# Moving an in-place difference, a copy and a block of zeros in a matmul with logsumexp

## The chip, the cores and the metric

The kernel runs on one core of a Trainium2 chip. The metric is the device time of one execution in microseconds; of several runs the median is taken. A profiled execution gives, beside its time, the span from its first to its last instruction and a record of every instruction on each engine: TensorE (PE, its weight loads shown as PEld), VectorE (DVE), ScalarE (ACT), GpSimd (POOL) and SyncE (SP).

## The reference

```python
def setup_inputs():
    m, k, n = 1024, 4096, 4096
    return {
        "a": np.random.randn(m, k).astype(np.float32),
        "b": np.random.randn(k, n).astype(np.float32),
    }

def reference(a, b):
    x = np.matmul(a, b)
    return special.logsumexp(x, axis=-1).astype(np.float32)
```

A product of 1024 x 4096 by 4096 x 4096, of which only the logarithm of the sum of exponentials of each row is kept: 1024 numbers.

## The kernel before

**Tiles.** The 1024 rows are 8 row tiles of 128 (MT). K is 32 tiles of 128, taken in 16 pairs (KP): the two tiles of a pair are the two K halves of a 2x2 split. The 4096 columns are 8 blocks (NB) of 512 (FD), each split into two halves of 256 (H). Both inputs are loaded as f32 and turned to f16 by the loading DMA, issued by POOL. Each load of a block of b is cut into four groups of four K pairs (G, GI).

**Block 0** (column block 0) is computed in the ordinary way while a streams in. Pieces of a land in slots of the buffer tb, PE transposes them (L169), DVE and ACT take turns in copying the transposed pieces to aT (L180, L182), and `plain` multiplies them (L187) as soon as both sides are there. Beside this DVE forms sums of parts of a: s1 = A11+A22, s2 = A21+A22, s5 = A11+A12 (`a_sums_early`), and later, in place in aT, A21-A11 and A12-A22 (`a_sums_late`). At the very start `warm` issues filler matmuls on a block of zeros (L257), which lies in a part of s5 that isn't written yet; they produce nothing that is used.

**Blocks 1 to 7** use Strassen's seven products in place of eight. A *quad* is a pair of row tiles by one column block: four quads (MP) per block. The result of a quad lies in two PSUM tiles: r0 holds C11 and C12 side by side, r1 holds C21 and C22. The sums of parts of b are made by DVE once for each block, by the methods of `Block`, group by group:

| name | value | where |
|---|---|---|
| T1 | B11+B22 | tb |
| T4 | B21-B11 | tb |
| T6 | B11+B12 | tb |
| T7 | B21+B22 | in place of B21 |
| T3 | B12-B22 | in place of B12 |

In each quad PE runs M1 = s1 T1 into c11, M5 = s5 B22 into c12, M2 = s2 B11 into c21, M6 = (A21-A11) T6 into c22, then M7 = (A12-A22) T7 added to c11, M3 = A11 T3 added to c12, and M4 = A22 T4 added to c21, 16 matmuls of 256 columns each (L332). Before M7, M3 and M4 add to their PSUM halves, ACT has to copy what stands there: M1 and M5 together (L382, to e), M2 (L387, to s). After M3 and M4 ACT copies again (L420, L422), DVE subtracts and adds the copies crosswise (L78, L81), and takes the maximum of each row (L84). The exponentials with their sums (ACT, L89) wait in the list `pending` and are issued by `flush()` in the next quad, between the copies of M1, M5 and of M2.

The first two quads of block 1 are *joint*: their M1, M5, M2 and M6 are issued together, group by group, since the sums of block 1 come one group at a time. Each then goes its own way with M7, M3, M4. The second of them has a buffer e of its own.

**The turn from one block to the next.** In the last quad of a block (`tail`) DVE makes the next block's sums. T1 is issued before the additions of that quad, T6 before its M7, and T4, T7, T3 at the end, behind its maxima. T6 reads B12, T4 reads B21: T3 and T7 overwrite these, and so come later.

**Order.** The order of the instructions on every engine is the order of the program (a manual schedule); each engine works through its own queue in order, and a wait of one instruction holds up all that is queued behind it on the same engine.

The places that matter for the change, by name: `zeros` (L259) and `warm`; the choice of e (L347); the copies at L382 and L387; the tail's T6 (L416); and the tail's last loop (L433).

Of the kernel before, what the change touches and what calls it, by code (L numbers as in the profile page):

```python
# [13 lines left out]
def kernel(  # L14
# [6 lines left out]
    nc = tc.nc  # L21
    P = 128
    FD = 512
    H = FD // 2
    f32 = mybir.dt.float32
# [9 lines left out]
    MP, KP = MT // 2, KT // 2  # L35
    SC = 1024
    KC, JT = K // SC, SC // P
    G = 4
# [7 lines left out]
    fix_pool = ctx.enter_context(tc.tile_pool(name="fix", bufs=1))  # L46
# [9 lines left out]
            name=nc.get_next_instruction_name(),  # L56
# [10 lines left out]
    s5 = cst_pool.tile([P, KP, MP, P], f16, name="s5")  # L67
# [9 lines left out]
    def add(o, x, y):  # L77
        nc.vector.tensor_tensor(out=o, in0=x, in1=y, op=ALU.add)  # L78

    def sub(o, x, y):  # L80
        nc.vector.tensor_tensor(out=o, in0=x, in1=y, op=ALU.subtract)  # L81

    def lse_max(pt, m, nb):
        nc.vector.tensor_reduce(  # L84
            out=negmax[:, m, nb : nb + 1], in_=pt, axis=AX.X, op=ALU.max, negate=True
        )

    def lse_exp(pt, m, nb):
        nc.scalar.activation(  # L89
            out=pt,  # L90
            in_=pt,
            func=AF.Exp,
            bias=negmax[:, m, nb : nb + 1],
            scale=1.0,
            accum_out=tsum[:, m, nb : nb + 1],
        )

    def load_b(nb, g, parts=1):
        bt = bt_pool.tile([P, GI, 2, FD], f16, name=f"b_{nb}_{g}", tag="bt")
        step = 2 * GI // parts  # L100
        flat = bt.rearrange("p i t n -> p (i t) n")
        rows = b.rearrange("(k p) n -> p k n", p=P)
        for h in range(parts):
            nc.gpsimd.dma_start(  # L104
                out=flat[:, h * step : (h + 1) * step],
                in_=rows[:, g * 2 * GI + h * step : g * 2 * GI + (h + 1) * step, ts(nb, FD)],
            )
        return bt
# [33 lines left out]
    def acc_tiles(name):  # L142
        return [
            psum_pool.tile([P, FD], f32, name=f"acc_{name}_{h}", tag="ps")
            for h in range(2)
        ]
# [49 lines left out]
    def a_sums_early(r, q):  # L196
        a11, a12 = aT[:, r, 0, q, 0, :], aT[:, r, 1, q, 0, :]
        a21, a22 = aT[:, r, 0, q, 1, :], aT[:, r, 1, q, 1, :]
        add(s1[:, r, q], a11, a22)
        add(s2[:, r, q], a21, a22)  # L200
        add(s5[:, r, q], a11, a12)

    def a_sums_late(r, q):
        a11, a12 = aT[:, r, 0, q, 0, :], aT[:, r, 1, q, 0, :]
        a21, a22 = aT[:, r, 0, q, 1, :], aT[:, r, 1, q, 1, :]
        sub(a21, a21, a11)
        sub(a12, a12, a22)
# [48 lines left out]
        for _ in range(n):  # L256
            nc.tensor.matmul(acc[2][1], zeros[:, 0:P], zeros[:, 0:FD], start=True, stop=True)  # L257

    zeros = s5[:, 0].rearrange("p q c -> p (q c)")  # L259
    nc.vector.memset(zeros[:, 0:FD], 0.0)  # L260
    warm(10)
    blk = Block(1)
# [45 lines left out]
    def flush():  # L308
        for f in pending:
            f()  # L310
        pending.clear()

    for nb in range(1, NB):
        nxt = None
        if nb + 1 < NB:
            nxt = Block(nb + 1)
            for g in range(G):
                nxt.raw.append(load_b(nb + 1, g))
        quads = {}
        for q in range(MP):  # L320
            if q not in quads:

                both = (0, 1) if nb == 1 and q == 0 else (q,)
                for p in both:
                    quads[p] = acc_tiles(f"{nb}_{p}")
            r0, r1 = quads[q]
            c11, c12 = r0[:, 0:H], r0[:, H:FD]
            c21, c22 = r1[:, 0:H], r1[:, H:FD]

            def product(c, lhs, rhs, start=False, g=None):  # L330
                for i in range(KP) if g is None else range(g * GI, (g + 1) * GI):
                    nc.tensor.matmul(  # L332
                        c,
                        lhs(i),
                        rhs(i),
                        start=(start and i == 0),
                        stop=(i == KP - 1),
                        skip_group_check=True,
                    )

            first, tail = nb == 1 and q < 2, nxt is not None and q == MP - 1
            final = nxt is None and q == MP - 1


            s = fix_pool.tile([P, 4, H], f32, name=f"s_{nb}_{q}", tag="s")
            x, e = s[:, 1::2], s[:, 0:2]
            if final or (first and q == 1):  # L347
                e = fix_pool.tile([P, 2, H], f32, name=f"e_{nb}_{q}", tag="e")

            def m1(c, p=q, **k):  # L350
                product(c, lambda i: s1[:, i, p], lambda i: T1[:, i], **k)

            def m5(c, p=q, **k):
                product(c, lambda i: s5[:, i, p], lambda i: blk.b(i, 1, 1), **k)

            def m2(c, p=q, **k):
                product(c, lambda i: s2[:, i, p], lambda i: blk.b(i, 0, 0), **k)

            def m6(c, p=q, **k):
                product(c, lambda i: aT[:, i, 0, p, 1], lambda i: T6[:, i], **k)  # L360

            def m7(c, **k):
                product(c, lambda i: aT[:, i, 1, q, 0], lambda i: blk.b(i, 1, 0), **k)

            def m3(c, **k):
                product(c, lambda i: aT[:, i, 0, q, 0], lambda i: blk.b(i, 0, 1), **k)

            def m4(c, **k):
                product(c, lambda i: aT[:, i, 1, q, 1], lambda i: T4[:, i], **k)

            if first and q == 0:
                for g in range(G):
                    for p in both:
                        u0, u1 = quads[p]
                        m1(u0[:, 0:H], p=p, start=True, g=g)
                        m5(u0[:, H:FD], p=p, g=g)
                        m2(u1[:, 0:H], p=p, start=True, g=g)
                        m6(u1[:, H:FD], p=p, g=g)
            elif not first:
                m1(c11, start=True)  # L380
                m5(c12)
            nc.scalar.copy(out=e, in_=r0.rearrange("p (h n) -> p h n", h=2))  # L382
            flush()
            if not first:
                m2(c21, start=True)
                m6(c22)
            nc.scalar.copy(out=s[:, 2], in_=c21)  # L387
            if tail:
                for g in range(G):
                    nxt.do_t1(g)  # L390
            add(s[:, 2], s[:, 2], e[:, 1])
            sub(s[:, 0], s[:, 2], e[:, 0])
            if final:

                z = psum_pool.tile([P, FD], f32, name="z", tag="ps")[:, 0:H]
                y = e[:, 0]
                m3(c12)
                nc.scalar.copy(out=x[:, 0], in_=c12)
                nc.scalar.copy(out=y, in_=c11)
                m4(c21)  # L400
                nc.scalar.copy(out=x[:, 1], in_=c21)
                m7(z, start=True)
                sub(x[:, 0], x[:, 0], s[:, 0])
                sub(y, y, s[:, 2])
                lse_max(c12, 2 * q, nb)
                lse_exp(c12, 2 * q, nb)
                add(c22, c22, x[:, 0])
                lse_max(r1, 2 * q + 1, nb)
                lse_exp(r1, 2 * q + 1, nb)
                add(y, y, x[:, 1])  # L410
                add(z, z, y)
                lse_max(z, 2 * q, NB)
                lse_exp(z, 2 * q, NB)
                continue
            if tail:
                for g in range(G):  # L416
                    nxt.do_t6(g)
            m7(c11)
            m3(c12)
            nc.scalar.copy(out=x[:, 0], in_=c12)  # L420
            m4(c21)
            nc.scalar.copy(out=x[:, 1], in_=c21)  # L422
            sub(x, x, s[:, 0::2])
            add(c22, c22, x[:, 0])
            add(c11, c11, x[:, 1])
            rows = (r0, r1)
            for h in range(2):
                lse_max(rows[h], 2 * q + h, nb)
                pending.append(lambda h=h, q=q, nb=nb, rows=rows: lse_exp(rows[h], 2 * q + h, nb))
            if first and q == 1:  # L430
                a_sums_early(slice(0, KP), MP - 1)
                a_sums_late(slice(0, KP), MP - 1)
            if tail:  # L433
                for f in (nxt.do_t4, nxt.do_t7, nxt.do_t3):
                    for g in range(G):
                        f(g)
        blk = nxt
# [42 lines left out]
```

## Time and profile before

| what | value |
|---|---|
| median of three runs | 440.37 us (439.47 to 440.76) |
| profiled execution, its own time | 438.74 us |
| its span | 436.8 us |
| granted TensorE clock | 0.999 |
| PE busy | 426.1 us, 98% of the span |
| DVE busy | 228.2 us, 52% |
| ACT busy | 109.6 us, 25% |
| first product of block 1 | 83.7 us after the start |
| moved by DMA | 42.48 MB |

How to read it: the spans and starts given below are microseconds from the first instruction of the profiled execution. Matmuls are pipelined, so the duration of one runs over the start of the next; distances between starts are the better measure. The profile names a tile by its name in the program and a buffer number; several names are shortened in it: s_69, s_70 and s_71 are s1, s2 and s5; acc_0_0 and acc_0_1 are r0 and r1 of quad 0 of a block, acc_1_0 and acc_1_1 those of quad 1, and so on, and b_0 to b_3 are the four groups of a block of b.

### The profile page before, as it was taken

What the parts mean: (1) busy time and instruction counts of PE and PEld (TensorE: products, weight loads), DVE (VectorE), ACT (ScalarE), POOL (GpSimd) and SP (SyncE); (2) the same over time, 40 slices, a digit from 0 to 9 for tenths busy, and PEclk for the clock granted to TensorE, in tenths of its full rate; (3) what the DMA queues carried; (4) which work ended last, traced back from release to release, by engine and by line L of the source; (5) the groups of instructions that cost most, each with busy time, mean ns of one, the idle gap of its engine ahead of it and who ended that gap; (6) DMA issues with size and microseconds to landing.
All of it is one profiled execution on the core that took longest, in us unless ns stands there. A gap on an engine that the chain in (4) does not pass through costs nothing.

```text
span 436.8 us, 8377 instructions
## 1 busy us (share of the span) xinstructions
PE 426.1 (98%) x3679; PEld 349.3 (80%) x3679; DVE 228.2 (52%) x434; ACT 109.6 (25%) x262; POOL 54.0 (12%) x84
## 2 busy tenths in 40 slices
PE   7999999999999999999999999999999999999995
PEld 3455555687888888888888888888888888888884
DVE  0336456943868533683358632693348722693324
ACT  2121226203222211222222212222222122222223
POOL 7444440200003000300003000300003000000000
PEclk9999999999999999999999999999999999999999
DMA  8999999998009910397009920298008930000000
GB/s 130 208 208 207 208 209 207 207 207 141 2 0 161 208 21 0 50 207 132 2 0 146 207 36 0 36 207 146 2 0 130 207 52 0 2 2 2 0 2 1
DMA packets 38260, 42.48 MB, mean 97 GB/s; under 512 B 1360, under 2 KB 34128, under 8 KB 38224
## 3 DMA queue, kind: packets, MB, share of 16 engines
q0 software_dynamic: 38080, 41.95, 57.1%
q8 instruction: 28, 0.46, 0.4%
q14 instruction: 8, 0.07, 0.0%
q1 hardware_dynamic: 144, 0.00, 0.0%
HBM read 83.89 MB, written 0.00 MB: 192 GB/s over the span
## 4 chain that ended last, share of the span: by engine, by line
PE 94%; DMA 2%; ACT 1%; DVE 1%; POOL 1%; issue 0%; POOLq 0%; DVEq 0%
PE acc_0_0_2998 L332 2%; PE acc_0_0_3538 L332 2%; PE acc_0_0_2458 L332 2%; PE acc_0_0_1378 L332 2%; PE acc_0_0_4070 L332 2%; PE acc_0_0_1918 L332 2%; PE acc_1_0_836 L332 2%; PE acc_1_79 L187 2%; PE acc_2_0_4326 L332 2%; PE acc_3_0_3382 L332 2%; PE acc_2_0_1634 L332 2%; PE acc_3_0_3922 L332 2%; PE acc_2_0_3794 L332 2%; PE acc_3_0_2842 L332 2%; PE acc_1_0_2586 L332 2%; PE acc_3_0_2302 L332 2%
## 5 line engine op out<-in xcount | busy, mean ns | idle before, releaser
L332 PEld LDWEIGHTS <-aT 128*128 128x128 f16 x1792 | 175.2, 98 | 25.6 <-issue 5.5
L332 PEld LDWEIGHTS <-s_69 128*128 128x128 f16 x448 | 43.8, 98 | 5.3
L332 PEld LDWEIGHTS <-s_70 128*128 128x128 f16 x448 | 43.8, 98 | 5.1
L332 PEld LDWEIGHTS <-s_71 128*128 128x128 f16 x448 | 43.8, 98 | 5.1
L187 PEld LDWEIGHTS <-aT 128*128 128x128 f16 x256 | 23.7, 98 | 24.8 <-ACT aT L182 1.2
L180 DVE COPY aT<-tps_84 128x1024 f16<-128x1024 f16 x16 | 11.1, 691 | 42.2 <-PE tps_84 L169 42.2
L182 ACT COPY aT<-tps_85 128x1024 f16<-128x1024 f16 x16 | 16.2, 1011 | 53.4 <-PE tps_85 L169 53.4
L169 PEld LDWEIGHTS <-tb 128*128 128x128 f16 x256 | 17.0, 98 | 10.1 <-DMA tb<-in_a_dram 3.0
L158 POOL DMA_DIRECT2D tb<-in_a_dram x32 | 17.5, 548 | 21.1 <-DMA tb<-in_a_dram 12.1
L257 PE MATMUL acc_1_83<-s_71 128*128 128x512 f16 x31 | 9.8, 461 | 1.9 <-DVE s_71 L260 1.2
L81 DVE TENSOR_TENSOR aT<-aT 128x512 f16<-128x512 f16 (+1 forms) x26 | 11.3, 481 | 0.0
L169 PE MATMUL tps_85<-ident,tb 128*128 128x128 f16 x128 | 9.8, 219 | 1.3 <-DMA tb<-in_a_dram 1.3
L169 PE MATMUL tps_84<-ident,tb 128*128 128x128 f16 x128 | 9.9, 220 | 0.4 <-DMA tb<-in_a_dram 0.4
L257 PEld LDWEIGHTS <-s_71 128*128 128x128 f16 x31 | 3.1, 112 | 5.9 <-issue 2.2
L104 POOL DMA_DIRECT2D b_0_1910<-in_b_dram x1 | 0.9, 881 | 46.0 <-PE acc_3_0_1762 L332 46.0
L104 POOL DMA_DIRECT2D b_0_2450<-in_b_dram x1 | 0.9, 878 | 46.1 <-PE acc_3_0_2302 L332 46.1
L104 POOL DMA_DIRECT2D b_0_3530<-in_b_dram x1 | 0.9, 878 | 46.1 <-PE acc_3_0_3382 L332 46.1
L104 POOL DMA_DIRECT2D b_0_2990<-in_b_dram x1 | 0.9, 878 | 46.0 <-PE acc_3_0_2842 L332 46.0
L104 POOL DMA_DIRECT2D b_0_1370<-in_b_dram x1 | 0.9, 873 | 45.0 <-PE acc_3_0_1222 L332 45.0
L78 DVE TENSOR_TENSOR s_71<-aT 128x512 f16<-128x512 f16 (+1 forms) x13 | 6.3, 481 | 0.0
L78 DVE TENSOR_TENSOR s_70<-aT 128x512 f16<-128x512 f16 (+1 forms) x13 | 6.3, 481 | 0.0
L78 DVE TENSOR_TENSOR s_69<-aT 128x512 f16<-128x512 f16 (+1 forms) x13 | 6.2, 478 | 0.0
(1008 smaller groups left out, 851.3 us busy)
## 6 DMA issues: line engine op xcount, KB each, us to landing
tb<-in_a_dram POOLq DMA_DIRECT2D x32, 256.0 KB, 9.6
b_0_104<-in_b_dram POOLq DMA_DIRECT2D x4, 256.0 KB, 6.9
b_1_115<-in_b_dram POOLq DMA_DIRECT2D x4, 256.0 KB, 10.1
b_2_138<-in_b_dram POOLq DMA_DIRECT2D x4, 256.0 KB, 9.8
b_3_267<-in_b_dram POOLq DMA_DIRECT2D x4, 256.0 KB, 9.8
b_0_539<-in_b_dram POOLq DMA_DIRECT2D x1, 1024.0 KB, 13.6
b_1_541<-in_b_dram POOLq DMA_DIRECT2D x1, 1024.0 KB, 17.4
b_2_543<-in_b_dram POOLq DMA_DIRECT2D x1, 1024.0 KB, 21.5
```

The source lines that it names most:

```text
L78: nc.vector.tensor_tensor(out=o, in0=x, in1=y, op=ALU.add)
L81: nc.vector.tensor_tensor(out=o, in0=x, in1=y, op=ALU.subtract)
L104: nc.gpsimd.dma_start(out=flat[:, h * step : (h + 1) * step], in_=rows[:, g * 2 * GI + h * step : g * 2 * GI + (h + 1) * step, ts(nb, FD)],)
L158: nc.gpsimd.dma_start(out=slot, in_=a_m[m, :, ts(kc, SC)])
L169: nc.tensor.matmul(pst[:, ts(j, P)], src[:, ts(j, P)], ident, is_transpose=True, start=(j == 0), stop=(j == JT - 1),)
L180: nc.vector.tensor_copy(out=dst, in_=v)
L182: nc.scalar.copy(out=dst, in_=v)
L187: nc.tensor.matmul(pt, aT[:, i, kp, m // 2, m % 2, :], blk0.raw[i // GI][:, i % GI, kp, :], start=(done[m] == 0), stop=(done[m] == KT - 1),)
L257: nc.tensor.matmul(acc[2][1], zeros[:, 0:P], zeros[:, 0:FD], start=True, stop=True)
L332: nc.tensor.matmul(c, lhs(i), rhs(i), start=(start and i == 0), stop=(i == KP - 1), skip_group_check=True,)
```

## The change

Three edits:

1. In the tail, T3 is issued right behind T6, ahead of the last quad's M7 and of its additions and maxima, and no longer behind T7.
2. The copy of M1 and M5 of the second joint quad is issued in the first joint quad, behind that quad's copy of M2, and not at the head of the second quad.
3. The zeros for the filler matmuls lie in the last K slice of s5 and not in the first.

```diff
-    zeros = s5[:, 0].rearrange("p q c -> p (q c)")
+    zeros = s5[:, KP - 1].rearrange("p q c -> p (q c)")
...
-            if final or (first and q == 1):
+            if final:
                 e = fix_pool.tile([P, 2, H], f32, name=f"e_{nb}_{q}", tag="e")
+            if first and q == 1:
+                e = e1
...
-            nc.scalar.copy(out=e, in_=r0.rearrange("p (h n) -> p h n", h=2))
+            if not (first and q == 1):
+                nc.scalar.copy(out=e, in_=r0.rearrange("p (h n) -> p h n", h=2))
             flush()
             if not first:
                 m2(c21, start=True)
                 m6(c22)
             nc.scalar.copy(out=s[:, 2], in_=c21)
+            if first and q == 0:
+                e1 = fix_pool.tile([P, 2, H], f32, name=f"e_{nb}_1", tag="e")
+                nc.scalar.copy(out=e1, in_=quads[1][0].rearrange("p (h n) -> p h n", h=2))
...
             if tail:
-                for g in range(G):
-                    nxt.do_t6(g)
+                for f in (nxt.do_t6, nxt.do_t3):
+                    for g in range(G):
+                        f(g)
             m7(c11)
             m3(c12)
...
             if tail:
-                for f in (nxt.do_t4, nxt.do_t7, nxt.do_t3):
+                for f in (nxt.do_t4, nxt.do_t7):
                     for g in range(G):
                         f(g)
```

With the new lines the copy of M2 stands at L390, the early copy at L393, and the copies behind M3 and M4 at L427 and L429.

## The prediction

> **What bounds the kernel now.** I read the page first, then the waits of TensorE (PE), then the chain of waits around one change of column block, then the timelines of DVE and ACT at the places that the diff touches.
>
> ```profile
> PE 426.1 (98%) x3679; PEld 349.3 (80%) x3679; DVE 228.2 (52%) x434; ACT 109.6 (25%) x262; POOL 54.0 (12%) x84
> PE 94%; DMA 2%; ACT 1%; DVE 1%; POOL 1%; issue 0%; POOLq 0%; DVEq 0%
> ```
>
> PE holds 94% of the chain that ended last. No matmul is added, removed or reordered, so all that the change can win is idle time on PE. The list of PE's waits names most of it:
>
> ```profile
> PE tps_85 L169 <- DMA tb<-in_a_dram: 1.3, 1, 1.3
> PE acc_1_83 L257 <- DVE s_71 L260: 1.2, 1, 1.2
> PE acc_1_0_836 L332 <- ACT e_1_1027 L382: 0.9, 1, 0.9
> PE acc_1_83 L257 <- DVE s_71 L78: 0.7, 1, 0.7
> ```
>
> The third and fourth lines are touched: the copy of M1 and M5 of the second joint quad, and the filler matmuls that read s5. The in-place B12-B22 isn't in this list, because its stalls come in slices under 0.2 us that the view puts to the weight loads as "issue". Two windows and the chain show them: the first quad of block 2, then the second.
>
> ```profile
> 134.05:146.93 12.88, 12.87 (x115) 10.94 (x113) 10.73 (x19) 3.06 (x8) 0.76 (x1) 1.00 1.24 206
> 146.93:159.15 12.22, 12.22 (x114) 10.95 (x113) 3.59 (x7) 3.05 (x8) 0.00 (x0) 1.00 0.71 118
> ```
>
> The same seven products take 12.88 us in the first quad of a block and 12.22 in the others, at full clock (1.00). DVE and PE at that place (DVE start, duration):
>
> ```profile
> 131.86 0.68 DVE L78 TENSOR_TENSOR tb<-b_3_832 128x1024 f16<-128x1024 f16 x1
> 134.49 0.69 DVE L81 TENSOR_TENSOR s_3_1224<-s_3_1224 128x512 f32<-128x512 f32 x1 [1.95 <-ACT s_3_1224 L422]
> ...
> 139.63 0.69 DVE L78 TENSOR_TENSOR b_0_826<-b_0_826 128x1024 f16<-128x1024 f16 x1
> 140.23 0.69 DVE L78 TENSOR_TENSOR b_1_828<-b_1_828 128x1024 f16<-128x1024 f16 x1
> ...
> 143.84 0.69 DVE L81 TENSOR_TENSOR b_3_832<-b_3_832 128x1024 f16<-128x1024 f16 x1
> 144.44 0.43 DVE L78 TENSOR_TENSOR s_0_1380<-s_0_1380 128x256 f32<-128x256 f32 x1
> ```
>
> ```profile
> 142.19 0.60 PE L332 MATMUL acc_0_0_1378<-b_3_832,aT 128*128 128x256 f16 x4
> 142.78 0.60 PE L332 MATMUL acc_0_0_1378<-b_0_826,aT 128*128 128x256 f16 x4
> 143.38 0.60 PE L332 MATMUL acc_0_0_1378<-b_1_828,aT 128*128 128x256 f16 x4
> ```
>
> M3 reads B12-B22 (T3). Its four groups start at 142.78, 143.38, 143.98 and 144.58, each 0.75 us after the start of "its" DVE instruction (142.03, 142.63, 143.24, 143.84). DVE makes a group every 0.60 us and PE uses one in 0.44 (16 matmuls in 1.75). Against a free start at 142.63, M3 loses 0.15+3x0.16 = 0.64 us. M7 before it, on T7, had no stall: 140.88, 141.31, 141.75, 142.19. The other five turns repeat this within 0.02 us, so DVE costs PE 6x0.64 = 3.9 us in all.
>
> **T3 moved (six turns).** Nothing is added or dropped: four DVE instructions per turn, spaced 0.60, i.e. 2.41 us of DVE. They leave the place behind T7 (142.03 to 144.44) and enter behind T6, where DVE stands idle for 1.95 us until ACT has copied M4. T3 would run from 132.46 to 134.87. The subtraction "s_3_1224 L81" behind it started at 134.49, so the gap is 0.38 us too short. Everything queued behind the T3s slips by 0.38: that subtraction, two additions, two maxima, four T4, four T7. Who waits for these?
>
> - ACT's exponentials of the old quad: they started at 138.11 behind another copy; the second maximum now ends at 137.31+0.38 = 137.69. Covered.
> - T4: M4 reads it at 144.4 and later, made by 140.1. Covered by M7 and M3.
> - T7, read by M7: this is late next. Starts become 140.01, 140.61, 141.21, 141.81; with 0.75 from DVE start to PE start, M7's groups can go at 140.76, 141.36, 141.96, 142.56. PE wants 140.88, 141.32, 141.75, 142.19, so the last group is 0.37 late. T7 had no slack in its last group (141.43+0.75 = 142.18).
>
> M3 then follows freely. The stall doesn't go; it moves from M3 to M7 and shrinks from 0.64 to 0.37. Gain 0.27 per turn, 6x0.27 = 1.6 us. DVE's later work (s_0_1380 at 144.44) comes earlier by 2 us, and nothing waits for it before 147.
>
> T3 now lies beside four POOL instructions that issue the loads of the block after next (131.31 to 134.80, 0.87 to 0.90 each). In the trace two T6s already start beside the first of them (131.26 and 131.86: 0.69 and 0.68 us, as elsewhere), and that POOL instruction takes 0.87 against 0.88 to 0.90 for those beside an idle DVE. So I charge nothing. The Trainium skill speaks against the move here ("SBUF — State Buffer", section "Who interferes with whom"): a DVE instruction with two SBUF inputs contends with a GpSimd instruction that reads SBUF, and whichever starts second is fully blocked. T3 is such an instruction. If the rule held for these issues, three of them (0.88 each) could hold DVE for up to 2.6 us per turn, 15.8 us in all; by the row it is 0. The page adds that it has seen no such stall between tensor_tensor and DMA issue, and the row is of the same shapes, so I take 0. POOL itself may be late without harm: the last of these loads lands at 133.9+21.4 = 155.3, first used at 174.62.
>
> **The copy of M1, M5 of the second joint quad (once).** The ACT copy (0.59 us) goes from 103.42, behind the two copies that wait for quad 0's M3 and M4, to right behind quad 0's M2/M6 copy (96.16 to 96.53). PE finishes the joint products at about 97.7, so it runs by about 98.4; ACT was idle there until 101.40. M7 of quad 1 can then start at 102.95 (M4 of quad 0 starts at 101.20 and issues for 1.75) instead of 104.06: 1.11 us. But what is late next? M4 of quad 1 writes c21, and must wait for the ACT copy of c21, which stands behind the two exponentials of quad 0:
>
> ```profile
> 105.93 0.66 ACT L89 ACTIVATE acc_0_0_834<-acc_0_0_834,negmax 128x512 f32<-128x512 f32 x1 [1.92 <-DVE negmax L84]
> ...
> 107.27 0.37 ACT L387 COPY s_1_1026<-acc_1_1_837 128x256 f32<-128x256 f32 x1
> ```
>
> The exponentials wait for DVE's maxima, which wait for M4 of quad 0; none of these moves. The c21 copy ends at 107.64, and M4 of quad 1 starts at 107.69 in the trace, 0.14 after M3 would have let it. With M7 and M3 1.11 us earlier, M4 still starts at 107.69; PE's wait only becomes 1.25 us there. Gain: 0. Bounds: 0 and 1.1.
>
> **The zeros for the filler matmuls (once).** They move from the first to the last K slice of s5. Before, the first write of s5 makes the next filler wait: PE had issued its last useful matmul at 12.58+2x0.216 = 13.01 and started again at 13.88, behind DVE's s5 (13.41+0.42). Now no wait. The useful matmuls behind it use b_0 rows that landed by 10.4. The next load needed is the transpose's: weight load at 15.19-0.87 = 14.32; POOL, waiting for that same landing, went on at 14.26. Later tiles have more than a microsecond to spare at each transpose, and from 13.88 to 84 the chain is PE, a few ACT copies that wait for PE, and no DMA. So the 0.87 us stays: gain 0.87, bounds 0 (DMA takes it back) and 0.9.
>
> **Sum.** 0.87+1.6+0 = 2.5 us. The profiled execution took 438.74 us (span 436.80, 1.94 around it); it becomes 436.2, span 434.3. That execution lies 1.6 us under the median of the three timed runs (440.37). Taken from the median: 437.9 us.
>
> **Rivals.**
>
> - *The full T3 stall goes* (T7 isn't late, as if the DVE gap were long enough): 3.9+0.9 = 4.7, 435.6 us. Against it: the gap is 1.95 and four T3 take 2.41, on rows that agree to 0.01 us. Chance 0.07.
> - *The joint copy also pays*: 2.5+1.1 = 3.6, 436.8 us. Against it: c21's copy ends at 107.64 whatever M7 does. Chance 0.08.
> - *Only the turns or only the start pays*: DMA takes back the filler's 0.87 (the fourth tile of a lands only about 0.1 us before it is wanted, by POOL's record), leaving 1.6, 438.8 us; or T7's lateness eats the turns' gain, leaving 0.9, 439.5 us. The latter needs each T3 to take 0.07 us more than T3 and T6 take now. Chance 0.11 and 0.08.
> - *Slower: POOL's DMA issues hold DVE during T3.* Place: between T6 and the subtraction at 134.49. Price: each 0.1 us that T3 ends later is 0.1 us more stall at M7, six times. One issue of 0.88 per turn blocking it gives a stall of 0.37+0.88 = 1.25 in place of 0.64, +3.7 us, less the start's 0.87: +2.8, 443.2 us. It decides when T3 is held for more than 0.63 us per turn (1.0 of stall: (1.0-0.64)x6 = 2.2, 1.3 above the start's 0.87). For it: the rule above. Against it: the T6 rows. Chance 0.04.
>
> **How the numbers follow.** The forecast itself has 0.62. A measurement of this kernel can tell about 0.3%, 1.3 us, from no change: faster is below 439.05. Forecast, the two better rivals and nearly all of the turns-only case (it lies just below that bound; I count two thirds) give 0.84 faster; the rest of that case and start-only 0.12; slower 0.04. The range goes from 436.4 (joint copy pays, a little more) to 439.2 (turns only): outside are the full gain below, start-only and slower above, some 0.19.
>
> **What would show it.** Right: the first quad of a block lasts 12.60 us, not 12.88; M7's last two groups start 0.60 apart and M3's 0.44; the subtraction behind T3 starts right behind it with no wait for ACT; T7's last instruction starts 0.38 later against the turn's M7; the joint M7 starts right behind M4 and M4 of quad 1 shows a wait for L390 of 1.2 us; the first fillers after s5 show no wait and block 1's first product starts near 83.0. Wrong: T3 rows longer than 0.69 or apart by more than 0.60; M4 of quad 1 starting before 107 us less the start's gain; a wait on tb's DMA at 14 us.

## The result, and the profile after

The changed kernel takes 436.7 us (median of four runs, 436.51 to 437.09) against 439.92 us for the kernel before in the same comparison: a ratio of 0.9927, 95% interval 0.9906 to 0.9949, so 2.2 to 4.1 us less. A second comparison with more runs of the kernel before gave 0.9947 (0.9935 to 0.9960), 1.8 to 2.9 us less. The predicted gain, 2.5 us, lies within both intervals. The predicted time, 437.9 us, lies above all four runs, because it was counted down from a median of three runs (440.37) that was high: in the later comparisons the kernel before took 438.69 to 439.16 us. The profiled execution after took 436.6 us, its span is 434.8 us.

The list of PE's waits after the change:

```profile
PE tps_85 L169 <- DMA tb<-in_a_dram: 2.4, 1, 2.4
PE acc_1_83 L257 <- DVE s_71 L260: 1.2, 1, 1.2
PE acc_1_1_837 L332 <- ACT s_1_1028 L390: 1.1, 1, 1.1
...
```

Two waits of before are gone: that of a filler matmul on s5 (0.7) and that of the second joint quad on the copy of M1 and M5 (0.9). A new one of 1.1 us stands in the third line, at the same quad: r1 (acc_1_1) waits for the copy of M2. And the wait for an early tile of a has grown from 1.3 to 2.4 us, which is no effect of the change: the third experiment shows how much this landing varies by itself.

The windows of the first quad of block 2 and of the second:

```profile
133.87:146.44 12.57, 12.56 (x114) 10.92 (x113) 9.13 (x17) 3.05 (x8) 0.74 (x1) 1.00 1.24 206
146.44:158.67 12.23, 12.23 (x115) 10.96 (x113) 3.59 (x7) 3.05 (x8) 0.00 (x0) 1.00 0.73 122
```

By these windows the first quad lost 0.31 us of its 12.88. By the starts of the first products, the better measure, it took 12.87 to 12.88 us before and takes 12.58 at each of the six turns after (12.58 to 12.59 in a second profiled execution), against 12.23 for the other quads: 0.29 us is won and 0.35 us of stall is left. DVE at that turn, from the last T6 to the subtraction behind T3, then the last T7s:

```profile
131.68 0.68 DVE L78 TENSOR_TENSOR tb<-b_3_832 128x1024 f16<-128x1024 f16 x1
132.28 0.68 DVE L81 TENSOR_TENSOR b_0_826<-b_0_826 128x1024 f16<-128x1024 f16 x1
...
134.08 0.68 DVE L81 TENSOR_TENSOR b_3_832<-b_3_832 128x1024 f16<-128x1024 f16 x1
134.69 0.68 DVE L81 TENSOR_TENSOR s_3_1224<-s_3_1224 128x512 f32<-128x512 f32 x1
...
141.01 0.69 DVE L78 TENSOR_TENSOR b_2_830<-b_2_830 128x1024 f16<-128x1024 f16 x1
141.62 0.69 DVE L78 TENSOR_TENSOR b_3_832<-b_3_832 128x1024 f16<-128x1024 f16 x1
```

The subtraction (134.69) carries no wait for ACT any more: it starts 0.61 us after the last T3, as soon as DVE is free. PE at M7 and at the start of M3:

```profile
140.69 0.60 PE L332 MATMUL acc_0_0_1378<-b_0_826,aT 128*128 128x256 f16 x4
141.15 0.60 PE L332 MATMUL acc_0_0_1378<-b_1_828,aT 128*128 128x256 f16 x4
141.75 0.60 PE L332 MATMUL acc_0_0_1378<-b_2_830,aT 128*128 128x256 f16 x4
142.35 0.60 PE L332 MATMUL acc_0_0_1378<-b_3_832,aT 128*128 128x256 f16 x4
142.79 0.60 PE L332 MATMUL acc_0_0_1378<-b_0_826,aT 128*128 128x256 f16 x4
143.23 0.60 PE L332 MATMUL acc_0_0_1378<-b_1_828,aT 128*128 128x256 f16 x4
```

M7's second, third and fourth groups start 0.60 us apart, at DVE's pace, the last two 0.74 and 0.73 us after T7's third and fourth instruction; M3's groups (from 142.79) follow every 0.44 us, at PE's own pace. The stall has moved from M3 to M7 and is smaller.

### The profile page after: what moved, and what is told of

It is laid out like the page before. It is cut to its first block, busy times and chain, and to the rows that moved or that the text cites. A ratio compares the mean times of both kernels' runs of the same rounds, so it can differ in the third digit from the quotient of the medians.

```text
span 434.8 us, 8371 instructions
## 1 busy us (share of the span) xinstructions
PE 423.8 (97%) x3679; PEld 349.1 (80%) x3679; DVE 227.7 (52%) x434; ACT 109.5 (25%) x262; POOL 54.1 (12%) x84
## 4 chain that ended last, share of the span: by engine, by line
PE 94%; DMA 2%; ACT 2%; DVE 1%; POOL 1%; issue 0%; DVEq 0%; POOLq 0%; ACTq 0%
DMA tb<-in_a_dram 2%; PE acc_1_79 L187 2%; PE acc_0_0_4070 L332 2%; PE acc_0_0_3538 L332 2%; PE acc_0_0_2998 L332 2%; PE acc_0_0_2458 L332 2%; PE acc_0_0_1918 L332 2%; PE acc_0_0_1378 L332 2%; PE acc_1_0_1506 L332 2%; PE acc_2_0_4326 L332 2%; PE acc_1_0_2586 L332 2%; PE acc_2_0_1094 L332 2%; PE acc_2_0_3794 L332 2%; PE acc_1_0_3666 L332 2%; PE acc_3_0_2842 L332 2%; PE acc_2_0_2174 L332 2%
```

## The experiments

All comparisons are against the kernel before, run beside each kernel on the same chip. In the traces of these kernels the profile names tiles without numbers (acc for every PSUM tile, s for s1, s2, s5 and the buffers of the quads). The first three take the change apart.

### T3 alone

```diff
             if tail:
-                for g in range(G):
-                    nxt.do_t6(g)
+                for f in (nxt.do_t6, nxt.do_t3):
+                    for g in range(G):
+                        f(g)
...
-                for f in (nxt.do_t4, nxt.do_t7, nxt.do_t3):
+                for f in (nxt.do_t4, nxt.do_t7):
```

> Only T3 behind T6; the copy and the zeros as before. Theory (T7 late in place of T3): the first quad of a block lasts 12.58 us as after the change, M7's last groups start 0.60 apart, all other distances as before; 6 x 0.29 = 1.7 us off the time of before. Rival (the measured 3.2 us comes from the turns alone, the trace of one execution being short of it): 3 us or more off.

Measured: 437.19 us against 438.69, ratio 0.9966 (0.9956 to 0.9977), 1.0 to 1.9 us less. The first quads of a block last 12.57 to 12.58 us, the joint quads 25.70 us from start to start as before. The turns are worth 1.7 us by the trace, and the time agrees; 3 us is excluded.

### The copy of M1, M5 alone

```diff
+            if first and q == 0:
+                e1 = fix_pool.tile([P, 2, H], f32, name=f"e_{nb}_1", tag="e")
+                nc.scalar.copy(out=e1, in_=quads[1][0].rearrange("p (h n) -> p h n", h=2))
```

(with the choice of e and the skipped copy in the second quad, as in the change)

> Only the early copy of M1, M5 of the second joint quad. Theory (the wait moves from M7 to M4 of that quad, behind the copy of c21): joint quads last 23.96 us from the second quad's first product to the next quad's, as before; PE waits 1.1 us at acc_1_1 for L390; time the same as before, within 0.3 us. Rival (the copy pays): 1.1 us off, 22.9 us for the joint quads.

Measured: 438.93 us against 438.69, ratio 1.0005 (0.9996 to 1.0014). PE's waits in this kernel:

```profile
PE acc L332 <- ACT s L390: 1.1, 1, 1.1
```

The wait for e (0.9 us at M7) has become a wait of 1.1 us for the copy of M2, at M4. The same place in the kernel before (M7, then M4 of the second joint quad) and in the changed kernel (M4):

```profile
104.06 0.60 PE L332 MATMUL acc_1_0_836<-b_0_539,aT 128*128 128x256 f16 x4 [0.95 <-ACT e_1_1027 L382]
...
107.69 1.91 PE L332 MATMUL acc_1_1_837<-tb,aT 128*128 128x256 f16 x16
```

```profile
107.50 1.91 PE L332 MATMUL acc_1_1_837<-tb,aT 128*128 128x256 f16 x16 [1.09 <-ACT s_1_1028 L390]
```

Counted from the first product of block 1 (83.73 before, 83.55 after), M4 starts 23.96 and 23.95 us later: the early copy did not move it. From the first product of the joint quads to the first product after them it takes 25.70 us, with the copy early or late.

### The zeros alone

```diff
-    zeros = s5[:, 0].rearrange("p q c -> p (q c)")
+    zeros = s5[:, KP - 1].rearrange("p q c -> p (q c)")
```

> Only the zeros in the last K slice. Theory: from the transpose of the third tile of a (its landing) to the first product of block 1 it takes 71.4 us against 72.3 before; 0.9 us off the time, on top of what that landing varies between executions. Rival (DMA takes the gain back): the same 72.3 us, or a new wait of PE for a tile of a behind it; no gain.

Measured: 437.52 us against 438.69, ratio 0.9976 (0.9966 to 0.9986), 0.6 to 1.5 us less. PE at the place itself, in the kernel before and then in this kernel:

```profile
11.48 0.62 PE L169 MATMUL tps_84<-ident,tb 128*128 128x128 f16 x8 [0.38 <-DMA tb<-in_a_dram]
...
13.88 0.82 PE L257 MATMUL acc_1_83<-s_71 128*128 128x512 f16 x3 [0.71 <-DVE s_71 L78]
```

```profile
11.76 0.62 PE L169 MATMUL tps<-ident,tb 128*128 128x128 f16 x8 [0.21 <-DMA tb<-in_a_dram]
...
13.30 0.81 PE L257 MATMUL acc<-s 128*128 128x512 f16 x3
```

The first line of each fence is the transpose of the third tile of a, which waits for the tile's landing. The fillers that wait for DVE's s5 in the kernel before start 2.40 us after it; here the same group starts 1.54 us after it. The distance to this landing is the measure to use, since the landing itself varies from one execution to the next. It is read as the start of the weight load that waits for it (11.47 in the kernel before); over the profiled executions of this study it came between 11.26 and 12.34 us. Counted from it, the first product of block 1 comes after

| zeros in | executions | landing to block 1 |
|---|---|---|
| first K slice | before; T3 alone; copy alone | 72.26, 72.27, 72.26 |
| last K slice | zeros alone; after (two); slip, the c21 copy and T6, T3 kernels, and both, below | 71.38 in six, 71.37 in the T6, T3 kernel |

So the gain is 0.88 to 0.90 us whichever executions are compared. In the profiled execution after, the landing came at 12.17 instead of 11.47, and 0.70 of the 0.88 us is hidden there: block 1 started at 83.55 instead of 83.73. That isn't the change's doing: POOL issues this tile's transfer at 4.59 us in the profiled executions before and after alike, the three executions with the zeros in the first slice show landings of 11.27 to 11.88, those with the last slice 11.26 to 12.34, and the earliest of all, 11.26, is the changed kernel's second profiled execution. Why the landing varies was not looked into.

### One DVE instruction more ahead of T3

On the changed kernel; the last of the four T6 instructions is issued twice:

```diff
             if tail:
+                nxt.do_t6(G - 1)
                 for f in (nxt.do_t6, nxt.do_t3):
```

> The changed kernel with one of the T6 instructions issued twice in each turn (0.60 us more of DVE ahead of T3, the result unchanged). Theory (everything behind T3 slips one for one, and T7 has no slack): M7's stall grows by 0.60 in each of six turns, the first quad of a block takes 13.2 us, time 3.6 us above the changed kernel, about as slow as before or slower. Rival (there is slack between T7 and M7, and the stall has another cause): 12.6 us stays, time within 0.5 us of the changed kernel.

Measured: 439.95 us, ratio to before 1.0031 (1.0015 to 1.0046). The changed kernel's ratio was 0.9947, so this one is 1.0031/0.9947 = 1.0084 of it, 3.7 us above. The first quads of a block take 13.18 to 13.19 us: 0.60 more. PE's M7 now waits for T7 already in its first group, at all six turns:

```profile
PE acc L332 <- DVE b L78: 1.8, 6, 0.3
```

T7 has no slack at M7: the 0.60 us that DVE loses ahead of it, PE loses too.

### The changed kernel again

> The changed kernel once more, for a narrower interval. Theory (turns 6 x 0.29 and start 0.88 add up, the copy is worth nothing): 2.6 us off the time of before, ratio 0.994. Rival (the 3.2 us of the first four runs is the true size, something is missing in the sum): ratio 0.9927, 3.2 us.

Measured: 436.54 us against 438.70, ratio 0.9947 (0.9935 to 0.9960), that is 2.3 us. 3.2 us lies outside; 2.6 lies inside. In this profiled execution the landing came at 11.26, and the span is 433.9: against before, 6x0.29+0.88 from the change and 0.21 from the landing make 2.83 of the 2.9 us.

### The copy of M2 ahead of the exponentials, in the joint quads

On the changed kernel:

```diff
-            flush()
             if not first:
+                flush()
                 m2(c21, start=True)
                 m6(c22)
             nc.scalar.copy(out=s[:, 2], in_=c21)
+            if first:
+                flush()
```

> The changed kernel, and in the second joint quad the copy of c21 is issued ahead of quad 0's exponentials. Theory (M4 of that quad waits for this copy behind the exponentials; the early copy of M1, M5 is worth something only with it): PE's wait of 1.1 us at acc_1_1 is gone, joint quads take 24.5 us from start to start in place of 25.7, 1.2 us below the changed kernel. Rival (M4 waits for DVE's additions on another path, or ACT's later copies become late): the wait stays or shows up at the next quad, no gain.

Measured: 434.95 us against 438.70, ratio 0.9912 (0.9898 to 0.9925). The joint quads take 24.45 us, 1.25 less, and PE no longer waits there. ACT, at the second joint quad:

```profile
104.31 0.37 ACT L390 COPY s<-acc 128x256 f32<-128x256 f32 x1 [1.68 <-DVE acc L78]
104.98 0.66 ACT L89 ACTIVATE acc<-acc,negmax 128x512 f32<-128x512 f32 x1 [0.30 <-DVE negmax L84]
```

The copy (L390) now runs while ACT would have waited for the maxima. So there were two waits on one path, and the early copy of M1, M5 removed only the first. The early copy of M2 without that of M1, M5 was not run. In the kernel before, M4 waited only 0.14 us beyond the end of M3, so by estimate from that trace it would have won about 0.14 us alone: nearly all of the gain needs both copies.

### T6 and T3 before the additions that wait for ACT

On the changed kernel:

```diff
             if tail:
-                for g in range(G):
-                    nxt.do_t1(g)
+                for f in (nxt.do_t1, nxt.do_t6, nxt.do_t3):
+                    for g in range(G):
+                        f(g)
...
-            if tail:
-                for f in (nxt.do_t6, nxt.do_t3):
-                    for g in range(G):
-                        f(g)
             m7(c11)
```

> The changed kernel, with T6 and T3 right behind T1 in each turn, ahead of the two additions of the last quad that wait for ACT. Theory (T3 overran DVE's gap by 0.36 us; T6 can start 1.7 us sooner, in the gap before those additions): the first quad of a block takes 12.23 us like the others, PE has no stall at M7 or M3, 6 x 0.35 = 2.1 us below the changed kernel. Rival (T6 has to wait for M6 of the old quad, and the late additions hold up the subtraction behind M4): the stall at M7 stays or grows, no gain or slower.

Measured: 433.78 us against 438.70, ratio 0.9887 (0.9871 to 0.9904). All quads but the joint ones last 12.22 to 12.23 us. The medians lie 2.8 us below the changed kernel's; the trace has 6x0.35 = 2.1 us of that, and the intervals of the two ratios are wide enough for the rest. DVE and then PE at the first turn:

```profile
128.95 2.49 DVE L81 TENSOR_TENSOR b<-b 128x1024 f16<-128x1024 f16 x4
131.35 0.42 DVE L78 TENSOR_TENSOR s<-s 128x256 f32<-128x256 f32 x1
131.81 0.43 DVE L81 TENSOR_TENSOR s<-s 128x256 f32<-128x256 f32 x1
133.48 0.69 DVE L81 TENSOR_TENSOR s<-s 128x512 f32<-128x512 f32 x1 [1.25 <-ACT s L426]
```

```profile
139.87 3.66 PE L332 MATMUL acc<-b,aT 128*128 128x256 f16 x32
143.36 1.91 PE L332 MATMUL acc<-tb,aT 128*128 128x256 f16 x16
```

The four T3s end early enough that the subtraction at 133.48 waits for ACT again, as in the kernel before, and M7 and M3 (one row of 32) take 3.49 us from start to M4's start, PE's own pace.

### Both, and fewer fillers

Both edits on the changed kernel:

> Both of these edits on the changed kernel. Theory: they add up, 1.2 + 2.1 = 3.3 us below the changed kernel, some 5.9 us below the kernel before, ratio 0.9865. Rival: one of them gives nothing.

Measured: 433.41 us against 438.70, ratio 0.9874 (0.9860 to 0.9887), 5.5 us less, the expected 5.9 within its interval. The trace shows both gains in full: joint quads 24.45 us, all other quads 12.22 to 12.23. Its landing, 12.34, was the latest of all profiled executions.

The last kernel has both edits too, and leaves out the nine fillers behind the third tile's transpose:

```diff
-        if kc == 0 and len(have_a[0]) < 3:
+        if kc == 0 and not have_b[0]:
             warm(3)
```

> The version with both edits, and the nine filler matmuls left out that stand behind the transpose of the third tile of a (three groups of three; they produce nothing that is used). Theory (behind that landing PE is the bound, the fillers lie on its path, until the fourth tile's landing, 2.5 us after the third, binds): of the 9 x 0.22 = 1.95 us about 0.4 come ahead of the fourth tile, where DMA allows no more, and the last group's 0.65 behind it, so 70.4 us from the third tile's transpose to block 1 in place of 71.4; 1.0 us below the version with both edits. Rival (without fillers the granted clock falls in the gaps, or DMA takes it all): 71.4 us or more, no gain.

Measured: 431.66 us against 439.16, ratio 0.9830 (0.9809 to 0.9851). From the landing to block 1 it takes 81.92-11.71 = 70.21 us, 1.17 less than with the fillers (70.4 was expected), and PE's granted clock is 9 tenths or more in every slice, as before. Here DMA does bind:

```profile
11.71 0.62 PE L169 MATMUL tps<-ident,tb 128*128 128x128 f16 x8 [0.20 <-DMA tb<-in_a_dram]
12.17 1.46 PE L187 MATMUL acc<-b,aT 128*128 128x512 f16 x6
14.23 0.62 PE L169 MATMUL tps<-ident,tb 128*128 128x128 f16 x8 [0.60 <-DMA tb<-in_a_dram]
```

The fourth tile's transpose starts 2.52 us after the third's and waits for its landing, so 0.78 of the 1.95 us of fillers was cover for DMA and 1.17 was on the path. (The profiled execution is 1.8 us shorter than that of the kernel with both edits; the other 0.6 is its earlier landing.) This version is the fastest of the study, 7.5 us (6.5 to 8.4) below the kernel before.

## Why the prediction was right

- **Where the T3 stall goes.** Predicted: from 0.64 at M3 to 0.37 at M7, 0.27 us per turn, the first quad at 12.60. Measured: 0.29 per turn, from 0.65 to 0.35, the quad at 12.58 to 12.59, the stall at M7's groups 0.60 apart. (Its sum 0.15+3x0.16 for M3's stall makes 0.63; the starts of the quads give 0.65.) The step that carried it was the comparison of DVE's gap (1.95 us, plus the last T6's end) with four T3s; T7's last instruction slipped from 0.55 to 0.93 us after M7's start, the predicted 0.38. The slip kernel showed that T7 passes each further delay on to PE, and the T6, T3 kernel that with no overrun there is no stall.
- **The joint copy worth nothing.** Predicted: 0, M4 of the second joint quad still waiting for the copy of M2. Measured: 25.70 us with and without it, and a wait of 1.1 us in the new place; 1.25 by the starts of the products (predicted 1.25). Moving that second copy too brought 1.25 us.
- **The zeros.** Predicted 0.87; measured 0.88 from the landing on. The predicted start of block 1 near 83.0 wasn't met in the profiled execution (83.55), and its span was 434.8, not 434.3: the prediction took the landing of the third tile as fixed, and it came 0.70 us later. No new wait for DMA appeared around 14 us, and it was less close than the prediction thought. It took POOL's next step (14.26) for the fourth tile's landing and saw 0.1 us to spare. POOL goes on 0.25 us after the landing where that can be seen (11.72 against 11.47 for the third tile). In the kernel with fewer fillers the fourth tile's weight load, waiting for its landing, starts 2.51 us after the third's; with the zeros alone it starts 2.84 us after, with no wait: some 0.3 us to spare.
- **T3 beside POOL's issues.** POOL's four instructions (0.87 to 0.90 us each) stood at 131.12 to 134.61 in the trace after, beside T6 and T3; T3 took 0.68 us and started every 0.60 us. At the sixth turn no loads are left to issue, and T3 is just as long there, 0.69 us, at the same distance of 0.60. A POOL row of the first turn, then two T3s of the sixth:

```profile
132.85 0.89 POOL L104 DMA_DIRECT2D b_2_1374<-in_b_dram  x1
```

```profile
378.58 0.69 DVE L81 TENSOR_TENSOR b_0_3530<-b_0_3530 128x1024 f16<-128x1024 f16 x1
379.19 0.69 DVE L81 TENSOR_TENSOR b_1_3532<-b_1_3532 128x1024 f16<-128x1024 f16 x1
```

If the rule of the Trainium skill that the prediction cites ("SBUF — State Buffer", "Who interferes with whom") reached these issues, up to 2.6 us per turn would have been lost; it was 0 for instructions of this shape beside these issues. Whether the issues read SBUF at all, as the rule asks, no run here shows. The slower rival rested on this and fell with it.

- **The sum.** 1.74+0.88 = 2.6 us by the parts, 2.5 predicted; 1.0 to 1.9 for T3, 0.6 to 1.5 for the zeros and -0.6 to 0.2 for the copy, as gains in time. The measured 436.7 us lies only 0.3 us above the lower end of the predicted range, 436.4. That end was meant for a joint copy that pays, which it did not; the time came so low because the starting median was high. What confirms the prediction is the three parts, each measured alone, and not the time itself.

## What to carry to other kernels

Before an instruction is moved into an idle gap, compare its time with the gap to a tenth of a microsecond, and find who has no slack among all that is queued behind it: an overrun of 0.38 us here left 0.35 us of a stall of 0.65. A wait that is removed is worth only what the next wait on the same path leaves; look for everything that the same instruction, and those behind it, would wait for next. The list of waits named only the first of two copies here. And place scratch data where its last reader comes long before the first real writer, or it ties two engines together.

## What was not expected of the hardware

The landing of the same early tile varied by 1.1 us between executions (11.26 to 12.34 us after the start), while the way from it to block 1 repeated to 0.01 us in kernels with the same start, and so did the length of each quad. A quarter of a per cent of this kernel's time is decided before its third tile is in; a gain of that size is read from the distance to the landing, not from the span.
